# Activation and product of the experts with over 64 tokens, taken before the transpose

## The chip, the cores and the metric

One core of one Trainium2 chip runs the whole program. The metric is the device time of one execution in microseconds (us). The kernel before takes 1499.08 us, the median of three runs (1498.29 to 1501.63). PE is TensorE, ACT is ScalarE, DVE is VectorE, POOL is GpSimd and SP is SyncE.

## What is computed

The reference is a decoder trunk of two layers on 256 tokens of width 1024. Each layer has a mixer (gated linear attention beside a state-space part) and a feed-forward part: dense in layer 0, and in layer 1 eight experts of which every token uses two. The change touches the experts alone:

```python
def swiglu(t, w_gate, w_up, w_down):
    return (jax.nn.silu(t @ w_gate) * (t @ w_up)) @ w_down

def moe_swiglu(h, router_w, w_gate, w_up, w_down):
    ...
    for e in range(N_EXPERTS):
        out = out + gates[:, e:e + 1] * swiglu(t, w_gate[e], w_up[e], w_down[e])
```

`w_gate` and `w_up` of an expert are 1024 x 3584, `w_down` is 3584 x 1024, all float32.

## The kernel before

Products run in float32 accuracy out of split operands: a value is held as a high part and a low part, and PE multiplies high by high, low by high and high by low. So each weight that a DMA brings has to be split: ACT copies the high part (line 182) and DVE subtracts it for the low part (line 183), on tiles of 128 x 2048 elements, one megabyte. One such tile is an *item* here.

An expert's hidden width of 3584 is worked through in seven chunks of 512 columns. A chunk takes six items: two of the gate (G), two of the up projection (U), and two of the down projection (D), which belong to the chunk before, for its hidden values are ready only then. `moe_order` gives this order, G G U U D D. For each item `whole` takes the split weights, `mm_slots` issues the matmuls, `done` gives the buffers back, and `fill` inside it records the splits of a later item on ACT and DVE. Ten buffers of the split weights hold five items, so ACT and DVE work up to five items ahead of PE. Unsplit weights have seven buffers of their own by then, which SP's DMA queue refills when DVE has finished with one (line 154 issues the loads).

Every engine runs its own queue in the order in which the program was written. An engine waits at an instruction, and all that stands behind it waits too.

The tokens of an expert stand in slots, up to 128 of them. Which tokens go where is known only at run time, and so is their count. With at most 64 tokens (*narrow*) the slots hold high and low parts side by side and two matmuls do for three; with more (*wide*) three are issued. `modal` (lines 1192 to 1200) writes both versions into the program as the bodies of `tc.If` and its Else, and a register of PE, ACT and DVE chooses between them. The registers are loaded for PE, ACT and DVE in `is_narrow`.

G and U accumulate in PSUM with slots as rows and hidden columns as columns; D needs them the other way round. So after the second item of G or U, four things follow for each chunk, put by `put` behind certain items:

- `copy` (behind the last G and the last U item): ACT copies the accumulator to a tile `gs` or `us` in SBUF (line 1249).
- `gate` (behind the last U item): PE turns `gs` in four 128 x 128 pieces into `pt`, in a wide expert by transposes (line 1259), in a narrow one by a product with `fold`, which also adds the high and low rows (line 1257). ACT writes silu of it to `fsg` (line 1277).
- `hidden` (two items later): PE turns `us` likewise into `mm`; DVE multiplies it into `fsg` (line 1287).
- `parted` (one item later): ACT copies the high part of `fsg` into `fth` (line 1297), and DVE subtracts for the low part (line 1298).

`at` puts other work between the items: the gathering of the next expert's tokens, the combination of the last expert's output.

Of the kernel before, what the change touches and what calls it, by code (L numbers as in the profile page):

```python
# [8 lines left out]
F = mybir.dt.float32  # L9
# [4 lines left out]
AF = mybir.ActivationFunctionType  # L14
OP = mybir.AluOpType
AX = mybir.AxisListType

P = 128
# [4 lines left out]
FC = 512  # L23
# [8 lines left out]
HALF = P // 2  # L32
# [18 lines left out]
def trunk(ctx: ExitStack, tc: tile.TileContext, a: dict, out: bass.AP):  # L51
    nc = tc.nc
    pe, dve, act, pool, sp = nc.tensor, nc.vector, nc.scalar, nc.gpsimd, nc.sync

    const = ctx.enter_context(tc.tile_pool(name="const", bufs=1))
# [7 lines left out]
    def nm(s):  # L63
        uid[0] += 1
        return f"{s}_{uid[0]}"

    def ps_mm():
        return psum.tile([P, 512], F, name=nm("mm"), tag="mm", bufs=3)

    def ps_t():  # L70
        return psum.tile([P, 512], F, name=nm("pt"), tag="t", bufs=1)
# [6 lines left out]
    def ps_pair():  # L78
        turn[0] ^= 1
        return [ps_y(turn[0]), ps_y(turn[0])]  # L80
# [252 lines left out]
    pe.transpose(pt[:, :DK], c_rows, ident[:DK, :DK])  # L333
    act.activation(s_col, pt[:, :DK], AF.Silu)

    tri = const.tile([P, P], F, name="tri")
    dve.tensor_scalar(tri, jp, 0.0, None, op0=OP.is_ge)
    btri = const.tile([P, P], F, name="btri")
    dve.tensor_scalar(btri, jp, 0.0, 1.0 / 16.0, op0=OP.is_ge, op1=OP.mult)
    dve.memset(btri[0:64, 64:128], 0.0)  # L340
    bmask = btri.bitcast(I32)
# [850 lines left out]
    def modal(narrow, body):  # L1192

        if narrow is None:
            body(False)
        else:
            with tc.If(narrow == 1) as cmp:
                body(True)
            with cmp.Else():
                body(False)  # L1200
# [38 lines left out]

    def run_experts(mo, experts, operand, fold, at):  # L1240

        gs, us, sil, th, ys, ops = {}, {}, {}, {}, {}, {}
        due, ps = {}, {}
        order = list(moe_order(experts))
        where = {t: n for n, t in enumerate(order)}

        def copied(tag, p):
            out = mo.tile([P, FC], F, name=nm(tag), tag=tag)
            act.activation(out, p, AF.Copy)  # L1249
            return out  # L1250

        def folded(src, nar, p):

            for k in range(4):
                ks = slice(k * P, (k + 1) * P)
                if nar:
                    pe.matmul(p[:, ks], src[:, ks], fold, start=True, stop=True)
                else:
                    pe.transpose(p[:, ks], src[:, ks], ident)
            return p  # L1260

        def blocks(t, nar):
            return t.rearrange("p (k t) -> p k t", k=4)[:, :, :HALF if nar else P]

        def put(n, f, *args):
            due.setdefault(n, []).append((f, args))

        def copy(kind, key):
            (gs if kind == "G" else us)[key] = copied("gs" if kind == "G" else "us", ps.pop((kind,) + key))

        def gate(key):
            src, p = gs.pop(key), ps_t()
            s = sil[key] = mo.tile([P, FC], F, name=nm("fsg"), tag="fsg")

            def body(nar):
                folded(src, nar, p)
                act.activation(blocks(s, nar), blocks(p, nar), AF.Silu)

            modal(ops[key[0]][2], body)

        def hidden(key):
            src, p, s = us.pop(key), ps_mm(), sil[key]

            def body(nar):
                folded(src, nar, p)
                sv = blocks(s, nar)
                dve.tensor_tensor(sv, blocks(p, nar), sv, op=OP.mult)

            modal(ops[key[0]][2], body)

        def parted(key):
            t = th[key] = mo.tile([P, 4, P, 2], R, name=nm("fth"), tag="fth", bufs=2)
            s = sil.pop(key)

            def body(nar):
                sv, tv = blocks(s, nar), t[:, :, :HALF if nar else P]
                act.activation(tv[:, :, :, 0], sv, AF.Copy)
                dve.tensor_tensor(tv[:, :, :, 1], sv, tv[:, :, :, 0].bitcast(F), op=OP.subtract)

            modal(ops[key[0]][2], body)  # L1300

        for n, (kind, e, c, i) in enumerate(order):
            key = (e, c)
# [22 lines left out]
            modal(narrow, lambda nar: mm_slots(dsts, nar))  # L1326
            done()
            if kind in "GU" and i:
                put(n, copy, kind, key)
            if (kind, i) == ("U", 1):  # L1330
                lag = 1 if key == (experts[-1], NFC - 1) else 2
                put(n, gate, key)
# [54 lines left out]
    def moe(mo, ys, row, mT):  # L1387
# [8 lines left out]
        pr = mo.tile([P, 2, 2], F, name="pr")  # L1396
# [11 lines left out]
        pool.memset(onesb, 1.0)  # L1408
        iota_s = mo.tile([P, P], F, name="iota_s")
        pool.iota(iota_s, pattern=[[1, P]], base=0, channel_multiplier=0, allow_small_or_imprecise_dtypes=True)  # L1410
        iota_h = mo.tile([P, P], F, name="iota_h")
        pool.iota(iota_h, pattern=[[1, HALF], [0, 2]], base=0, channel_multiplier=0, allow_small_or_imprecise_dtypes=True)
        fold = mo.tile([P, P], F, name="fold")
        pool.iota(fold, pattern=[[-2, P]], base=0, channel_multiplier=1, allow_small_or_imprecise_dtypes=True)
        pm2 = mo.tile([P, 2, P], F, name="pm2")
        dve.tensor_scalar(pm2[:, 0], fold, 0.0, None, op0=OP.is_ge)
# [5 lines left out]
        key = mo.tile([P, NE], F, name="key")  # L1422
# [318 lines left out]

        acc = fnw = None
        y = run_experts(mo, list(range(NE)), lambda e: (xg[e % 2],) + narrow[e], fold, at)
        extra.remove("xm")
        sq, write = finisher(fnw)
# [109 lines left out]
    with tc.tile_pool(name="ffn", bufs=1) as fp:  # L1855
# [4 lines left out]
        ys = [ps_pair(), ps_pair()]  # L1860
# [14 lines left out]
    with tc.tile_pool(name="moe", bufs=1) as mo:  # L1875
        moe(mo, py, g1, mT)
# [23 lines left out]
```

## Time and profile before

| | |
|---|---|
| runs | 1499.08 us median, 1498.29 to 1501.63 |
| the profiled execution | 1499.08 us, of which the span is 1497.3 us |
| mean granted clock of PE | 0.984 |
| busy share of the span | PE 93%, DVE 86%, ACT 70%, POOL 3% |
| read from HBM | 480.12 MB, 321 GB/s over the span |

The span is the time from the first to the last recorded instruction of the profiled execution, so 1.8 us of its time lie outside it. Busy times of different instructions of one engine overlap at their ends, and ends of matmuls are modelled, so a share of 93% or 100% does not say that the engine could do no more. The experts' stage begins near 570 us and ends at the end. In the trace each expert can be told by its lines: 1257 is run in narrow experts only, 1259 in wide ones only.

### The profile page before, as it was taken

The numbers are of one execution on the slowest core, as the hardware profiler recorded it, in microseconds if no ns is written. First come the engines' busy times: TensorE is split into PE (matmuls) and PEld (weight loads), VectorE is DVE, ScalarE is ACT, GpSimd is POOL, SyncE is SP. The second block draws the span as 40 slices with busy tenths as digits, with TensorE's granted clock in tenths as the row PEclk, the third lists the DMA queues.
The fourth block names the chain that finished last, engine by engine and source line by source line (L and its number), as shares of the span: only waits on it lengthen the run. The fifth ranks groups of instructions, "written<-read, shape, count | busy, mean of one in ns | idle before, by whom it ended". The sixth has DMA issues, their size and how long they took to land.

```text
span 1497.3 us, 22117 instructions
## 1 busy us (share of the span) xinstructions
PE 1399.2 (93%) x7578; PEld 1197.3 (80%) x7578; DVE 1289.2 (86%) x1186; ACT 1051.8 (70%) x1255; POOL 46.0 (3%) x72
## 2 busy tenths in 40 slices
PE   4998899999999997999999999999999999998986
PEld 3876699999879776878888778888787888877765
DVE  7898877777766659999889999888999988999996
ACT  3474644544557557898778888778898778888875
POOL 2011000000010011000000000000000000000001
PEclk9999999999999999999999999999999999999998
DMA  9974778888854456999999999999999999999993
GB/s 335 302 259 142 260 268 310 320 314 316 297 176 141 146 175 221 344 395 392 394 340 371 392 392 395 393 348 366 391 393 392 394 371 361 387 393 395 392 393 143
DMA packets 204618, 483.29 MB, mean 323 GB/s; under 512 B 13119, under 2 KB 15405, under 8 KB 204462
## 3 DMA queue, kind: packets, MB, share of 16 engines
q1 hardware_dynamic: 203890, 480.05, 87.3%
q8 instruction: 99, 1.62, 0.4%
q10 hardware_dynamic: 428, 0.63, 0.1%
q0 software_dynamic: 144, 0.52, 0.1%
q14 instruction: 57, 0.47, 0.1%
HBM read 480.12 MB, written 1.05 MB: 321 GB/s over the span
## 4 chain that ended last, share of the span: by engine, by line
PE 70%; DVE 11%; DMA 7%; issue 6%; ACT 5%; POOL 1%; DVEq 0%; ACTq 0%; POOLq 0%
PE mm L1213 10%; PE y L1213 6%; PE mm L1209 5%; PE mm L1210 5%; PE mm L1207 5%; PE mm L429 4%; PE mm L430 4%; PE mm L428 4%; PE y L428 3%; PE y L430 3%; PE y L429 3%; PE y L1207 3%; PE y L1209 3%; DVE ws L183 3%; PE y L1210 3%
## 5 line engine op out<-in xcount | busy, mean ns | idle before, releaser
L174 ACT ACTIVATE ws<-raw 128x1024 fp32r<-128x1024 f32 x136 | 143.8, 1061 | 135.4 <-PE mm L430 62.5
L183 DVE TENSOR_TENSOR ws<-raw,ws 128x2048 fp32r<-128x2048 f32 x97 | 221.4, 2284 | 16.5 <-ACT ws L182 16.3
L175 DVE TENSOR_TENSOR ws<-raw,ws 128x1024 fp32r<-128x1024 f32 x136 | 164.3, 1221 | 55.9 <-ACT ws L174 55.5
L182 ACT ACTIVATE ws<-raw 128x2048 fp32r<-128x2048 f32 x97 | 185.7, 1915 | 25.6 <-PE mm L1210 12.4
L1209 PE MATMUL mm<-ws,hTl 128*128 128x512 f32 x336 | 134.9, 402 | 0.0
L1210 PE MATMUL mm<-ws,hTl 128*128 128x512 f32 x336 | 132.5, 394 | 0.0
L1207 PE MATMUL mm<-ws,hTh 128*128 128x512 f32 x448 | 124.2, 399 | 4.9 <-ACT gs L1249 2.7
L1213 PE MATMUL y<-ws,fth 128*128 128x512 f32 x448 | 126.4, 405 | 0.0
L1213 PE MATMUL mm<-ws,hTl 128*128 128x512 f32 x448 | 122.1, 394 | 0.0
L1213 PE MATMUL mm<-ws,hTh 128*128 128x512 f32 x448 | 121.2, 392 | 0.0
L367 DVE SCALAR_TENSOR_TENSOR ada<-raw,s_col,ada 128x1024 f32<-128x1024 f32 (+1 forms) x98 | 114.4, 1167 | 2.1
L183 DVE TENSOR_TENSOR ws<-xm,ws 128x2048 fp32r<-128x2048 f32 x46 | 105.1, 2285 | 11.5 <-ACT ws L182 11.3
L183 DVE TENSOR_TENSOR ws<-xx,ws 128x2048 fp32r<-128x2048 f32 x47 | 107.3, 2284 | 8.8 <-ACT ws L182 8.7
L183 DVE TENSOR_TENSOR ws<-ada,ws 128x2048 fp32r<-128x2048 f32 x47 | 107.4, 2285 | 7.5 <-ACT ws L182 6.9
L183 DVE TENSOR_TENSOR ws<-xce,ws 128x2048 fp32r<-128x2048 f32 x47 | 107.3, 2284 | 6.6 <-ACT ws L182 6.5
L183 DVE TENSOR_TENSOR ws<-q,ws 128x2048 fp32r<-128x2048 f32 x47 | 107.3, 2283 | 4.4 <-ACT ws L182 3.9
L428 PE MATMUL mm<-hTh,ws 128*128 128x256 f32 x384 | 108.1, 281 | 0.0
L429 PE MATMUL mm<-hTh,ws 128*128 128x256 f32 x384 | 106.9, 278 | 0.0
L430 PE MATMUL mm<-hTl,ws 128*128 128x256 f32 x384 | 106.9, 278 | 0.0
L1213 PEld LDWEIGHTS y<-ws,fth 128*128 128x128 f32 x448 | 88.9, 198 | 19.7
L182 ACT ACTIVATE ws<-q 128x2048 fp32r<-128x2048 f32 x47 | 90.1, 1917 | 16.0 <-PE mm L1210 7.1
L182 ACT ACTIVATE ws<-xx 128x2048 fp32r<-128x2048 f32 x47 | 90.1, 1917 | 16.0 <-PE mm L1210 4.9
(391 smaller groups left out, 3272.5 us busy)
## 6 DMA issues: line engine op xcount, KB each, us to landing
raw<-in_ada_w SPq DMA_DIRECT2D x48, 1024.0 KB, 5.7
raw<-in_moe_w_up SPq DMA_DIRECT2D x33, 1024.0 KB, 6.9
raw<-in_moe_w_gate SPq DMA_DIRECT2D x32, 1024.0 KB, 9.6
raw<-in_moe_w_down SPq DMA_DIRECT2D x32, 1024.0 KB, 12.3
raw<-in_w_in SPq DMA_DIRECT2D x21, 1024.0 KB, 5.3
ada<-in_moe_w_down SPq DMA_DIRECT2D x17, 1024.0 KB, 9.4
xx<-in_moe_w_gate SPq DMA_DIRECT2D x16, 1024.0 KB, 8.1
q<-in_moe_w_gate SPq DMA_DIRECT2D x16, 1024.0 KB, 12.9
```

What stands on the lines that cost most here:

```text
L174: act.activation(h, src, AF.Copy)
L175: dve.tensor_tensor(lo, src, h.bitcast(F), op=OP.subtract)
L182: act.activation(h, r, AF.Copy)
L183: low = lambda: dve.tensor_tensor(lo, r, h.bitcast(F), op=OP.subtract)
L367: dve.scalar_tensor_tensor(acc, w, s_col[:, k:k + 1], acc, op0=OP.mult, op1=OP.add)
L428: pe.matmul(ps, xh, wh, start=start, stop=False)
L429: pe.matmul(ps, xl, wh, start=False, stop=False)
L430: pe.matmul(ps, xh, wl, start=False, stop=stop)
L1207: pe.matmul(ps, xs[:, 0:HALF].rearrange("p s two -> p (s two)"), wh, start=start, stop=False)
L1209: pe.matmul(ps, xs[:, :, 0], wh, start=start, stop=False)
L1210: pe.matmul(ps, xs[:, :, 1], wh, start=False, stop=False)
L1213: pe.matmul(ps, both if nar else xs[:, :, 0], wl, start=False, stop=stop)
```

## The change

In a wide expert silu is taken and the product is formed with slots as rows, straight out of the accumulators, and one tile is transposed where two were. `gate_rows` and `up_rows` take the place of `copy`: behind the last G item ACT writes silu of the accumulator to `gs`, and behind the last U item DVE multiplies the accumulator of U by `gs` into a new tile `prod`. `gate` does nothing in a wide expert. `hidden` transposes `prod`, and `parted` splits it out of PSUM, which `hid` holds until then. In a narrow expert the same instructions run as before, but each step now stands in a `modal`, so that there are two more of these in each chunk. Two constant tiles, `iota_h` and `fold`, take the place of `tri` and `btri`, which are no longer needed by then, for room.

```diff
@@ -333,9 +333,9 @@
     pe.transpose(pt[:, :DK], c_rows, ident[:DK, :DK])
     act.activation(s_col, pt[:, :DK], AF.Silu)
 
-    tri = const.tile([P, P], F, name="tri")
+    tri = const.tile([P, P], F, name="tri", tag="tri")
     dve.tensor_scalar(tri, jp, 0.0, None, op0=OP.is_ge)
-    btri = const.tile([P, P], F, name="btri")
+    btri = const.tile([P, P], F, name="btri", tag="btri")
     dve.tensor_scalar(btri, jp, 0.0, 1.0 / 16.0, op0=OP.is_ge, op1=OP.mult)
     dve.memset(btri[0:64, 64:128], 0.0)
     bmask = btri.bitcast(I32)
@@ -1239,15 +1239,10 @@
 
     def run_experts(mo, experts, operand, fold, at):
 
-        gs, us, sil, th, ys, ops = {}, {}, {}, {}, {}, {}
+        gs, us, sil, hid, prod, th, ys, ops = {}, {}, {}, {}, {}, {}, {}, {}
         due, ps = {}, {}
         order = list(moe_order(experts))
         where = {t: n for n, t in enumerate(order)}
-
-        def copied(tag, p):
-            out = mo.tile([P, FC], F, name=nm(tag), tag=tag)
-            act.activation(out, p, AF.Copy)
-            return out
 
         def folded(src, nar, p):
 
@@ -1265,35 +1260,54 @@
         def put(n, f, *args):
             due.setdefault(n, []).append((f, args))
 
-        def copy(kind, key):
-            (gs if kind == "G" else us)[key] = copied("gs" if kind == "G" else "us", ps.pop((kind,) + key))
+        def gate_rows(key):
+
+            p = ps.pop(("G",) + key)
+            t = gs[key] = mo.tile([P, FC], F, name=nm("gs"), tag="gs")
+            modal(ops[key[0]][2], lambda nar: act.activation(t, p, AF.Copy if nar else AF.Silu))
+
+        def up_rows(key):
+
+            p, g = ps.pop(("U",) + key), gs[key]
+            t = us[key] = mo.tile([P, FC], F, name=nm("us"), tag="us")
+            w = prod[key] = mo.tile([P, FC], F, name=nm("pr"), tag="prod")
+
+            def body(nar):
+                if nar:
+                    act.activation(t, p, AF.Copy)
+                else:
+                    dve.tensor_tensor(w, p, g, op=OP.mult)
+
+            modal(ops[key[0]][2], body)
 
         def gate(key):
             src, p = gs.pop(key), ps_t()
-            s = sil[key] = mo.tile([P, FC], F, name=nm("fsg"), tag="fsg")
+            s = sil[key] = mo.tile([P, 4, HALF], F, name=nm("fsg"), tag="fsg")
 
             def body(nar):
-                folded(src, nar, p)
-                act.activation(blocks(s, nar), blocks(p, nar), AF.Silu)
+                if nar:
+                    folded(src, nar, p)
+                    act.activation(s, blocks(p, nar), AF.Silu)
 
             modal(ops[key[0]][2], body)
 
         def hidden(key):
-            src, p, s = us.pop(key), ps_mm(), sil[key]
+            src, w, s = us.pop(key), prod.pop(key), sil[key]
+            p = hid[key] = ps_mm()
 
             def body(nar):
-                folded(src, nar, p)
-                sv = blocks(s, nar)
-                dve.tensor_tensor(sv, blocks(p, nar), sv, op=OP.mult)
+                folded(src if nar else w, nar, p)
+                if nar:
+                    dve.tensor_tensor(s, blocks(p, nar), s, op=OP.mult)
 
             modal(ops[key[0]][2], body)
 
         def parted(key):
             t = th[key] = mo.tile([P, 4, P, 2], R, name=nm("fth"), tag="fth", bufs=2)
-            s = sil.pop(key)
+            s, p = sil.pop(key), hid.pop(key)
 
             def body(nar):
-                sv, tv = blocks(s, nar), t[:, :, :HALF if nar else P]
+                sv, tv = s if nar else blocks(p, nar), t[:, :, :HALF if nar else P]
                 act.activation(tv[:, :, :, 0], sv, AF.Copy)
                 dve.tensor_tensor(tv[:, :, :, 1], sv, tv[:, :, :, 0].bitcast(F), op=OP.subtract)
 
@@ -1326,7 +1340,7 @@
             modal(narrow, lambda nar: mm_slots(dsts, nar))
             done()
             if kind in "GU" and i:
-                put(n, copy, kind, key)
+                put(n, gate_rows if kind == "G" else up_rows, key)
             if (kind, i) == ("U", 1):
                 lag = 1 if key == (experts[-1], NFC - 1) else 2
                 put(n, gate, key)
@@ -1408,9 +1422,9 @@
         pool.memset(onesb, 1.0)
         iota_s = mo.tile([P, P], F, name="iota_s")
         pool.iota(iota_s, pattern=[[1, P]], base=0, channel_multiplier=0, allow_small_or_imprecise_dtypes=True)
-        iota_h = mo.tile([P, P], F, name="iota_h")
+        iota_h = const.tile([P, P], F, name="iota_h", tag="btri")
         pool.iota(iota_h, pattern=[[1, HALF], [0, 2]], base=0, channel_multiplier=0, allow_small_or_imprecise_dtypes=True)
-        fold = mo.tile([P, P], F, name="fold")
+        fold = const.tile([P, P], F, name="fold", tag="tri")
         pool.iota(fold, pattern=[[-2, P]], base=0, channel_multiplier=1, allow_small_or_imprecise_dtypes=True)
         pm2 = mo.tile([P, 2, P], F, name="pm2")
         dve.tensor_scalar(pm2[:, 0], fold, 0.0, None, op0=OP.is_ge)
```

Where one body of a `modal` gives an engine something to do and the other does not, the built program sets an event semaphore in the empty body: it waits until all that this engine has issued so far is finished, and then counts the engine's semaphore up by what the other body would have added. The listings below show that wait at the branch behind it, as `[waits DVE_49]` or `[waits PE_49]`. A row of the bodies stands for the narrow case first, then for the wide one. `L1197` is the branch of `modal`.

DVE behind the last U item of a chunk, before: a split, the branch of `gate` in which DVE has nothing to do, two more splits, and the bodies of `hidden` (`ws` are split weights, `raw`, `ada` unsplit ones).

```order
L183 TENSOR_TENSOR ws_5961<-raw_731_5674,ws_5960 128x2048 [waits DMAHW4_49,PE_49,Activation_49]
L1197 COMPARE_AND_BRANCH
L1197 UNCONDITIONAL_BRANCH x4
L183 TENSOR_TENSOR ws_6003<-ada_5706,ws_6002 128x2048 [waits DMAHW5_49,PE_49,Activation_49]
L183 TENSOR_TENSOR ws_6030<-raw_739_5733,ws_6029 128x2048 [waits DVE_49,DMAHW6_49,PE_49,Activation_49]
L1197 COMPARE_AND_BRANCH
L1287 TENSOR_TENSOR fsg_5969<-mm_6035,fsg_5969 128x4x64 [waits DVE_49,PE_49]
L1197 UNCONDITIONAL_BRANCH
L1287 TENSOR_TENSOR fsg_5969<-mm_6035,fsg_5969 128x512 [waits DVE_49,PE_49]
L1197 UNCONDITIONAL_BRANCH x2
```

And now: `up_rows` stands between (the row of line 1279 is the wide body, the branch with the wait above it the narrow one).

```order
L183 TENSOR_TENSOR ws_5960<-raw_733_5672,ws_5959 128x2048 [waits DVE_49,DMAHW4_49,PE_49,Activation_49]
L1197 COMPARE_AND_BRANCH
L1197 UNCONDITIONAL_BRANCH [waits DVE_49]
L1279 TENSOR_TENSOR pr_5966<-mm_5910,gs_5881 128x512
L1197 UNCONDITIONAL_BRANCH
L1197 COMPARE_AND_BRANCH
L1197 UNCONDITIONAL_BRANCH x4
L183 TENSOR_TENSOR ws_6000<-ada_5706,ws_5999 128x2048 [waits DVE_49,DMAHW5_49,PE_49,Activation_49]
L183 TENSOR_TENSOR ws_6027<-raw_741_5733,ws_6026 128x2048 [waits DMAHW6_49,PE_49,Activation_49]
L1197 COMPARE_AND_BRANCH
L1301 TENSOR_TENSOR fsg_5971<-mm_6032,fsg_5971 128x256 [waits DVE_49,PE_49]
L1197 UNCONDITIONAL_BRANCH
L1197 UNCONDITIONAL_BRANCH [waits DVE_49]
```

The multiplication moved up from behind the second D item, two splits earlier, and is in the wide body alone; at its new place the narrow body holds the wait for DVE's own work, and at its old place, line 1301, the wide body holds one.

PE behind the last U item of a chunk of expert 1, before: the last matmuls of U, the bodies of `gate`, and the branch to the first D item.

```order
L1213 MATMUL mm_6761<-ws_6654,hTl_6110 128x512 [waits DVE_49]
L1213 MATMUL mm_6761<-ws_6654,hTl_6110 128x512 x3
L1197 UNCONDITIONAL_BRANCH
L1197 COMPARE_AND_BRANCH
L1257 MATMUL pt_6818<-fold,gs_6759 128x128 [waits PE_49,Activation_49]
L1257 MATMUL pt_6818<-fold,gs_6759 128x128 x3
L1197 UNCONDITIONAL_BRANCH
L1259 MATMUL pt_6818<-ident,gs_6759 128x128 [waits PE_49,Activation_49]
L1259 MATMUL pt_6818<-ident,gs_6759 128x128 x3
L1197 UNCONDITIONAL_BRANCH
L1197 COMPARE_AND_BRANCH
```

And now.

```order
L1213 MATMUL mm_6756<-ws_6648,hTl_6108 128x512 [waits DVE_49]
L1213 MATMUL mm_6756<-ws_6648,hTl_6108 128x512 x3
L1197 UNCONDITIONAL_BRANCH
L1197 COMPARE_AND_BRANCH
L1197 UNCONDITIONAL_BRANCH x2
L1197 COMPARE_AND_BRANCH
L1252 MATMUL pt_6816<-fold,gs_6752 128x128 [waits PE_49,Activation_49]
L1252 MATMUL pt_6816<-fold,gs_6752 128x128 x3
L1197 UNCONDITIONAL_BRANCH
L1197 UNCONDITIONAL_BRANCH [waits PE_49]
L1197 COMPARE_AND_BRANCH
```

The four transposes of the wide body are gone, and the wait of PE for its own matmuls stands in their place, right ahead of the branch to the first D item.

## Rows read from the trace of the kernel before

**Rows 1.** Busy time by stretch: us, busy of each engine (instructions), clock, DMA share, GB/s.

```profile
700.00:800.00 100.00, 100.00 (x473) 84.63 (x472) 85.22 (x56) 75.30 (x63) 0.00 (x0) 1.00 1.00 368
806.00:906.00 100.00, 95.58 (x478) 79.32 (x477) 99.69 (x69) 87.99 (x78) 0.00 (x0) 0.98 1.04 392
1271.00:1371.00 100.00, 97.23 (x485) 81.22 (x484) 97.41 (x68) 85.37 (x76) 0.74 (x1) 0.98 1.04 391
1371.00:1471.00 100.00, 87.98 (x401) 69.95 (x399) 96.73 (x65) 82.00 (x65) 0.00 (x0) 0.95 1.03 390
```

**Rows 2.** Tile gs: instructions that read it, count, duration in ns, first and last start.

```profile
L1257 PE MATMUL pt<-fold,gs x280: 270/275/422, 577.9 to 1474.0; 128*128 128x128 f32 x140
L1259 PE MATMUL pt<-ident,gs x84: 270/272/273, 684.3 to 1256.6; 128*128 128x128 f32 x84
```

**Rows 3.** Waits in 806 to 906 us: us in total, times, longest.

```profile
ACT fth L1297 <- DVE fsg L1287: 10.7, 5, 2.8
PEld pt L1257 <- ACT gs L1249: 6.0, 5, 2.5
DVE ws L183 <- ACT ws L182: 0.2, 1, 0.2
```

**Rows 4.** Timeline of DVE, expert 2: start, us, idle before it in brackets.

```profile
859.79 2.28 DVE L183 TENSOR_TENSOR ws<-xce,ws 128x2048 fp32r<-128x2048 f32 x1
861.99 2.27 DVE L183 TENSOR_TENSOR ws<-raw,ws 128x2048 fp32r<-128x2048 f32 x1
864.19 0.41 DVE L1287 TENSOR_TENSOR fsg<-mm,fsg 128x256 f32<-128x256 f32 x1
```

**Rows 5.** Timeline of PE, expert 1, last U item to first D item.

```profile
699.10 1.09 PE L1213 MATMUL mm<-ws,hTl 128*128 128x512 f32 x4
700.04 0.60 PE L1259 MATMUL pt<-ident,gs 128*128 128x128 f32 x4
700.39 0.49 PE L1209 MATMUL y<-ws,fth 128*128 128x512 f32 x1
700.72 0.40 PE L1210 MATMUL y<-ws,fth 128*128 128x512 f32 x1
```

**Rows 6.** Timeline of DVE at the end, and line 1647: its event semaphores (DVEq is DVE's queue).

```profile
1487.44 0.14 DVE L1646 TENSOR_SCALAR fr<-fss 128x1 f32<-128x1 f32 x1
1487.69 0.31 DVE L1647 SCALAR_TENSOR_TENSOR fr<-fss,fr 128x1 f32<-128x1 f32 x1
...
L1647 DVEq EVENT_SEMAPHORE  x2: 21/21/21, 1487.6 to 1488.7; - x2
```

**Rows 7.** Line 1197 in DVE's queue: whole span, 856.0 to 856.5 us; line 183, 856.4.

```profile
L1197 DVEq COMPARE_BRANCH  x295: 43/47/63, 581.5 to 1479.2; - x148
...
L1197 DVEq COMPARE_BRANCH  x2: 43/45/47, 856.1 to 856.2; - x2
...
L183 DVEq EVENT_SEMAPHORE  x1: 50/50/50, 856.4 to 856.4; - x1
```

**Rows 8.** PE at 609 us: timeline of its weight loads, and line 1197 in its queue.

```profile
609.54 0.40 PEld L1599 LDWEIGHTS y<-ident,pm 128*128 128x128 f32 x2 [0.67 <-DVE pm L1577]
610.14 0.76 PEld L1207 LDWEIGHTS y<-ws,fth 128*128 128x128 f32 x4 [0.20 <-issue]
...
L1197 PEldq COMPARE_BRANCH  x2: 63/118/174, 609.8 to 610.0; - x2
```

**Rows 9.** PE's queue in expert 1: line 1197, and line 1259 behind it.

```profile
L1197 PEldq COMPARE_BRANCH  x1: 207/207/207, 702.8 to 702.8; - x1
...
L1259 PEldq EVENT_SEMAPHORE  x1: 51/51/51, 703.1 to 703.1; - x1
```

**Rows 10.** Timeline around 850 us: a product on DVE, and ACT, which waits for it.

```profile
849.28 0.42 DVE L1287 TENSOR_TENSOR fsg<-mm,fsg 128x256 f32<-128x256 f32 x1
...
849.79 0.44 ACT L1297 ACTIVATE fth<-fsg 128x256 fp32r<-128x256 f32 x1 [2.72 <-DVE fsg L1287]
850.12 1.89 ACT L182 ACTIVATE ws<-xm 128x2048 fp32r<-128x2048 f32 x1
```

## The prediction

> **What bounds the kernel now.** I read the busy time by stretch first, then the waits of one stretch, then the timelines of DVE and PE there. The reader is to see two kinds of stretch in the experts' stage. In wide experts PE is busy 100 of 100 us and DVE 85 [rows 1]; matmuls follow each other every 0.23 us with no gap between items [rows 5]. PE sets the time there. In narrow experts it is DVE: it is busy 99.7 of 100 us [rows 1], waited for ACT once, for 0.2 us [rows 3], and its splits follow each other every 2.20 us, though one takes 2.28 [rows 4]. The others wait behind it: ACT 10.7 us for DVE's product, and PE, through ACT's copy of gs, 6.0 us [rows 3]. The DMA engines look full in both kinds of stretch (share 1.00 to 1.04), but no wait of [rows 3], in the narrow one, is for a DMA, so that a later DVE there makes a later end. There are 84 / 4 = 21 wide chunks, three experts, and 280 / 8 = 35 narrow ones, five experts [rows 2]. The wide ones are experts 1, 3 and 5; 6 and 7 are both narrow and come last.
>
> **What the change removes.** In each wide chunk four transposes. The U item's last four matmuls begin at 699.10, the transposes 0.94 us later, the D item's first matmul 0.35 us after these, and its second one 0.33 us after the first where the last four of U stand 0.94 / 4 = 0.235 us apart [rows 5]. So four transposes cost 0.35 + 0.10 = 0.45 us of PE, and 21 x 0.45 = 9.45 us if nothing comes in their place. ACT loses a copy and a silu in each wide chunk, and DVE's product moves two items ahead, behind a split that is late anyway; in wide experts both engines have 15 us and more of room in 100 [rows 1], and the transposes of the product come two items later, so I cost this at nothing. What hides it is PE's bound; should DVE be late by more than the two items, PE would wait for the product. The narrow product, copies and folds stay as they are. DMA issues keep their order on SP and POOL.
>
> **What it adds: a wait of DVE for itself.** In a narrow chunk DVE now waits, behind the last U item, until its split has ended, and only then does its queue go on to the jump over the wide body, to the branch of gate with its own jump, and to the waits of the next split. Today the queue does such things while a split of 2.28 us runs, and nobody sees them: a compare or jump takes 43 to 63 ns [rows 7]. Behind a wait they are seen. Four prices, each from a row:
> - Lost overlap of two splits: 2.28 - 2.20 = 0.08 us [rows 4].
> - From the end of an instruction over an event semaphore that waits for it to the next start: 1487.58 to 1487.69, 0.11 us [rows 6].
> - A compare, a jump and the next entry of the queue: 856.1, 856.2 and 856.4, so 0.1 us for a compare that falls through and 0.2 for a jump that is taken [rows 7]. In the queue stand a jump, a compare and a jump: 0.5 us.
> - One more event semaphore ahead of the split, some 0.1 us by the same rows (an estimate from 0.11).
>
> Together 0.08 + 0.11 + 0.5 + 0.1 = 0.79, say 0.8 us. The lower bound is the wait alone, 0.19. For the upper one I take each entry at half as much again, 1.1. ACT's queue passes the branch behind its product and starts the next split 0.33 us behind the product's start [rows 10], which speaks for a smaller price, but that queue works beside an instruction of 0.44 us; I stay with DVE's own rows.
>
> All of DVE's time counts in experts 0, 2 and 4: 3 x 7 x 0.8 = 16.8 us. In experts 6 and 7, DVE has 2.6 and 3.3 us idle in 200 us [rows 1], a part of it waiting for weights; the delay uses this up first: 14 x 0.8 - 5.9 = 5.3 us.
>
> [...]
>
> **And a wait of PE for itself.** In a wide chunk the transposes' place is taken by a wait of PE for its own last matmul, with the branch to the D item behind it. The last of the four matmuls ends at 699.10 + 1.09 = 700.19 [rows 5]. From there: an instruction that waited for another engine starts some 0.09 us behind the end of what it waited for (ACT at 849.79, behind a product that ends at 849.28 + 0.42 = 849.70), the event semaphore takes 0.05 and its handing on some 0.02 [rows 9, 10], and a compare that jumps to the wide body has the next entry behind it after 0.3 us, nearer 0.27 by its length of 0.207 [rows 9]. That is 0.43, and the D item's first matmul begins at about 700.64, where it begins at 700.39 now: 0.25 us later, without the transposes. So what was removed is more than paid back. A second row bears this out: where PE's two small transposes at 609 us came late, the second weight load started at 609.80 and the D item's at 610.14, with a jump and a compare between, and 0.20 us of the time is put down to issue [rows 8]. Bounds: if only the 0.09 is seen, 0.11 us are won per chunk; with the branch at twice its price 0.5 us are lost. 21 x 0.25 = 5.2 us.
>
> **The sum.** 16.8 + 5.3 + 5.2 = +27.3 us. The profiled execution took 1499.08 us, 1497.3 of it the span; it is the median run itself, so the sum stands against either: 1526 us. With all prices at their lower bounds it is 21 x 0.19 - 21 x 0.11 = +1.7 us, with all at their upper ones 21 x 1.1 + (14 x 1.1 - 5.9) + 21 x 0.5 = +43 us.
>
> **Rivals.**
> - *Faster: waits of an engine for itself cost nothing.* Then the four transposes are won whole: 1499.1 - 9.45 = 1489.6 us. The point from which it decides is on PE: it wins only by as much as the next matmul starts sooner than 0.20 us behind the end of the last (700.39 - 700.19). For it: an engine runs its instructions in order anyway, and DVE's end-to-start is only 0.11 us [rows 6]. Against it: 0.08 us of overlap go in any case, and the entries behind the wait are in the rows. [...] 0.06.
> - *No change: only the waits are seen, the branches run ahead.* 0.19 on DVE and -0.11 on PE: +1.7 us, 1500.8. 0.08.
> - *Narrow experts are paced by the DMA engines, not DVE.* Their share is 1.04 there [rows 1]. Then DVE's delay is free in all of them, and PE's is left: +5.2 us, 1504.3. Against it: ACT, which reads the weights first, waits for DVE in [rows 3], and no wait there is for a DMA. 0.08.
> - *The entries of the queues cost half.* DVE's 0.6 us of them become 0.3, its delay 0.49; PE's branch costs 0.14 less, its delay 0.11: 21 x 0.49 + (14 x 0.49 - 5.9) + 21 x 0.11 = +13.6 us, 1512.7. For it speaks ACT's row [rows 10]. 0.18.
>
> That the change doesn't do what it says is no rival: the listing shows the transposes gone and both waits in place.
>
> **How the numbers follow.** The forecast has 0.60, the rivals 0.06, 0.08, 0.08 and 0.18. The range takes in the forecast but for its uppermost bounds, and the last two rivals, and leaves out the first two: 1504 to 1537 us, about 0.8. A measurement of this kernel can tell 0.2%, 3.0 us, from no change: faster 0.06, same 0.08, slower 0.86.
>
> **What the profile after would show.** If right: in wide chunks a gap of PE ahead of the first D matmul, which stands 700.39 - 699.10 = 1.29 us behind the first of the last four U matmuls now and would stand 1.54 behind it; in narrow chunks a gap of some 0.7 us on DVE behind the split that follows the last U item, put down to issue or to nothing; the time from product to product of expert 2, 864.19 - 849.28 = 14.91 us [rows 4, 10], 0.8 us longer; DMA share below 1.04 there. The prediction is wrong if DVE's narrow stretches show no such gap, if the gap is there and the experts are no longer for it, or if the D item's first matmul stands 1.29 us or less behind the U item's.

## The result and the profile after

The changed kernel takes 1525.79 us, the median of four runs, against 1499.93 us for the kernel before in as many: a ratio of 1.0178 (95% interval 1.0165 to 1.0190). It is slower by 25.9 us; 27 had been forecast. The profiled execution took 1528.11 us, with a span of 1526.3. Two executions, 2803 us of the kernel before and 2783 us of a later one (e9_fold), lie far outside all others and are in no ratio below.

Busy time by stretch, after, columns as in [rows 1]:

```profile
540.00:580.00 40.00, 37.20 (x198) 33.05 (x197) 27.02 (x50) 23.77 (x31) 1.12 (x2) 0.83 0.37 131
700.00:800.00 100.00, 97.78 (x444) 80.94 (x443) 85.25 (x58) 69.45 (x52) 0.00 (x0) 1.00 0.97 351
806.00:906.00 100.00, 95.55 (x471) 79.27 (x471) 94.17 (x64) 83.28 (x74) 0.00 (x0) 0.98 1.03 382
1371.00:1471.00 100.00, 90.93 (x411) 73.52 (x409) 95.50 (x67) 78.39 (x64) 0.74 (x1) 0.93 1.04 393
```

In the wide stretch PE falls from 100 to 97.8, in the narrow one DVE from 99.7 to 94.2: where each engine was the bound, it now has holes, and the clock in these two stretches is what it was (1.00 and 0.98). The holes stand where the listing had put the waits. The timeline of DVE in expert 2, and ACT beside it:

```profile
862.86 0.42 DVE L1301 TENSOR_TENSOR fsg<-mm,fsg 128x256 f32<-128x256 f32 x1
...
871.15 2.30 DVE L183 TENSOR_TENSOR ws<-q,ws 128x2048 fp32r<-128x2048 f32 x1
874.21 2.29 DVE L183 TENSOR_TENSOR ws<-xce,ws 128x2048 fp32r<-128x2048 f32 x1 [0.76 <-ACT ws L182]
876.42 2.29 DVE L183 TENSOR_TENSOR ws<-raw,ws 128x2048 fp32r<-128x2048 f32 x1
878.62 0.42 DVE L1301 TENSOR_TENSOR fsg<-mm,fsg 128x256 f32<-128x256 f32 x1
...
870.32 1.92 ACT L182 ACTIVATE ws<-xce 128x2048 fp32r<-128x2048 f32 x1
```

The brackets name ACT, but ACT's split of that tile ended at 870.32 + 1.92 = 872.24, two microseconds before DVE starts. What DVE did in the gap is in its queue, line 1197 (the branch and the wait in the empty body) and line 183 (the waits of the split itself):

```profile
L1197 DVEq COMPARE_BRANCH  x3: 43/47/47, 873.6 to 873.8; - x3
L1197 DVEq EVENT_SEMAPHORE  x1: 21/21/21, 873.5 to 873.5; - x1
...
L183 DVEq EVENT_SEMAPHORE  x2: 21/36/50, 874.0 to 874.1; - x2
```

The split ends at 873.45. The wait passes at 873.5, three branches follow from 873.6 to 873.8, two event semaphores at 874.0 and 874.1, and the next split starts at 874.21. PE in expert 1, with its queue:

```profile
708.57 1.09 PE L1213 MATMUL mm<-ws,hTl 128*128 128x512 f32 x4
710.12 0.51 PE L1209 MATMUL y<-ws,fth 128*128 128x512 f32 x1 [0.46 <-PEq L1197]
710.47 0.39 PE L1210 MATMUL y<-ws,fth 128*128 128x512 f32 x1
...
L1197 PEldq COMPARE_BRANCH  x2: 210/210/210, 709.9 to 710.2; - x2
L1197 PEldq EVENT_SEMAPHORE  x1: 51/51/51, 709.7 to 709.7; - x1
```

The four transposes of [rows 5] are gone, and the first D matmul stands 710.12 - 708.57 = 1.55 us behind the first of the last four U matmuls, where it stood at 1.29.

How much each expert lost is read from ACT, whose first write of `gs` in each marks its begin. For expert 1 and the one behind it, before and then after:

```profile
680.78 0.58 ACT L1249 ACTIVATE gs<-mm 128x512 f32<-128x512 f32 x1
806.44 0.58 ACT L1249 ACTIVATE gs<-mm 128x512 f32<-128x512 f32 x1
```

```profile
689.50 0.58 ACT L1267 ACTIVATE gs<-mm 128x512 f32<-128x512 f32 x1
817.08 0.58 ACT L1267 ACTIVATE gs<-mm 128x512 f32<-128x512 f32 x1
```

So 125.66 us before and 127.58 after. Worked out in the same way for all, from one profiled execution of each kernel (the last part reaches to the end of the span; the names are those of the experiments below):

| us | narrow 0, 2, 4 | wide 1, 3, 5 | 6, 7 to the end | sum |
|---|---|---|---|---|
| before | 313.8 | 377.9 | 228.4 | 920.0 |
| after | 330.7 | 383.4 | 231.5 | 945.6 |
| e6_idle | 329.5 | 375.3 | 233.6 | 938.4 |
| e1_tiny | 315.1 | 383.1 | 228.3 | 926.4 |
| e5_one | 325.6 | 382.0 | 228.3 | 935.9 |
| e3_gate | 330.0 | 368.5 | 228.8 | 927.2 |
| e8_before_gate | 319.3 | 375.1 | 227.7 | 922.1 |
| e2_splits | 315.3 | 383.2 | 228.5 | 927.0 |
| e4_both | 319.7 | 369.0 | 228.5 | 917.2 |
| e7_tiny_gate | 318.9 | 368.9 | 228.9 | 916.8 |
| e9_fold | 315.7 | 369.1 | 228.7 | 913.5 |
| e10_copy | 316.6 | 370.2 | 229.0 | 915.9 |
| e11_no_wait_dve | 315.2 | 370.7 | 229.5 | 915.4 |
| e12_no_wait | 314.7 | 368.8 | 228.1 | 911.6 |

The span grew by 29.0 us (1526.3 - 1497.3), the sum of this table by 25.5. The other 3.4 were lost ahead of the experts, in code whose work the change leaves alone. The mean clock differs there: 0.83 was granted from 540 to 580 us in the first row above, and 0.96 in the kernel before:

```profile
540.00:580.00 40.00, 35.02 (x207) 30.71 (x207) 28.82 (x49) 26.04 (x33) 1.12 (x2) 0.96 0.40 140
```

The experts began between 576.9 and 582.1 us in the fourteen traces, the kernel before at 577.3. The median run after is 2.3 us shorter than the profiled one. So the table is the closer measure of what an edit of the experts does, and medians are held against it. It is one execution of each kernel, though: the first D matmul of a wide chunk stands 1.29 us behind the first of the last four U matmuls in the kernel before, in e6_idle and in e8_before_gate alike, and their wide experts take 377.9, 375.3 and 375.1 us. Differences of 2 to 3 us in one column tell nothing by themselves.

### The profile page after: what moved, and what is told of

It reads as the page before. It is cut to its first block, busy times and chain, and to the rows that moved or that the text cites. A ratio compares the mean times of both kernels' runs of the same rounds, so it can differ in the third digit from the quotient of the medians.

```text
span 1526.3 us, 22692 instructions
## 1 busy us (share of the span) xinstructions
PE 1412.8 (93%) x7494; PEld 1200.8 (79%) x7494; DVE 1292.9 (85%) x1186; ACT 1029.5 (67%) x1213; POOL 44.4 (3%) x72
## 5 line engine op out<-in xcount | busy, mean ns | idle before, releaser
L1207 PE MATMUL mm<-ws,hTh 128*128 128x512 f32 x448 | 125.9, 403 | 2.2 <-ACT hTh L508 2.2
L1213 PE MATMUL mm<-ws,hTh 128*128 128x512 f32 x448 | 122.6, 396 | 0.0
```

Source lines behind the costliest of these rows:

```text
L1207: pe.matmul(ps, xs[:, 0:HALF].rearrange("p s two -> p (s two)"), wh, start=start, stop=False)
L1213: pe.matmul(ps, both if nar else xs[:, :, 0], wl, start=False, stop=stop)
```

## The experiments

Each ratio is that of the kernel's runs to those of the kernel before on the same chip, with its 95% interval.

### DVE's wait alone, in the kernel before

```diff
+        def idle_body(key):
+            w = mo.tile([P, 1], F, name=nm("one"), tag="one")
+            def body(nar):
+                if not nar:
+                    dve.memset(w, 0.0)
+            modal(ops[key[0]][2], body)
...
             if (kind, i) == ("U", 1):
...
+                put(n, idle_body, key)
                 put(n, gate, key)
```

> The kernel before, with one more modal behind the last U item: nothing in the narrow body, a memset of a 128x1 column on DVE in the wide one. So DVE waits for itself in narrow chunks as in the changed kernel, and nothing else is changed. Theory: the same gap of some 0.76 us in narrow chunks, 21 x 0.85 = 17.9 us in experts 0, 2 and 4, some 3 us in 6 and 7, nothing in wide ones: 1500 + 20 = 1520 us. Rival A (DMA engines pace the narrow experts): 1500 us. Rival B (only the wait is seen, 0.19 us): 1504 us.

Measured (e6_idle): 1518.96 us, ratio 1.0140 (1.0120 to 1.0160). Timeline of DVE in expert 2:

```profile
865.38 2.28 DVE L183 TENSOR_TENSOR ws<-q,ws 128x2048 fp32r<-128x2048 f32 x1
868.36 2.29 DVE L183 TENSOR_TENSOR ws<-xce,ws 128x2048 fp32r<-128x2048 f32 x1 [0.69 <-ACT ws L182]
```

The narrow experts 0, 2 and 4 take 15.8 us more, of 17.9 expected, 6 and 7 5.2 us, of 3 expected, and the wide ones lose nothing (375.3 against 377.9). No value is computed differently in this kernel, so the wait, with the branches behind it, alone makes most of the loss of the change. With the DMA engines as the bound of the narrow experts it would have been free; that rival falls.

### DVE's wait taken away

```diff
                 if nar:
                     act.activation(t, p, AF.Copy)
+                    dve.memset(w[:, 0:1], 0.0)
                 else:
                     dve.tensor_tensor(w, p, g, op=OP.mult)
```

> The narrow body of up_rows also gets one DVE instruction, a memset of a 128x1 column of the product's tile, so that DVE has work in both bodies and needs not wait for itself there. Theory (the wait of DVE for itself in narrow chunks costs 0.85 us a chunk, as the gap in the trace after): the gap of 0.76 us behind the split goes, about 0.1 to 0.15 us for the memset comes (an estimate from the 0.14 us of a 128x1 instruction), so about 20 us are given back but for 2 to 5: 1506 to 1511 us. Rival A (the time goes to the added branches, which stay, on three engines): no change, 1525 us. Rival B (DMA engines pace the narrow experts): no change either, though the gap on DVE goes.

Measured (e1_tiny): 1506.06 us, ratio 1.0044 (1.0029 to 1.0060). The branches are still there, and the narrow experts are back at 315.1 us (313.8 before); the wide ones keep their 383.1. The memset added nothing:

```profile
861.04 2.28 DVE L183 TENSOR_TENSOR ws<-xx,ws 128x2048 fp32r<-128x2048 f32 x1
...
865.45 2.28 DVE L183 TENSOR_TENSOR ws<-xce,ws 128x2048 fp32r<-128x2048 f32 x1
865.47 0.06 DVE L1278 MEMSET pr<- 128x1 f32 x1
867.66 2.28 DVE L183 TENSOR_TENSOR ws<-raw,ws 128x2048 fp32r<-128x2048 f32 x1
...
L1197 DVEq COMPARE_BRANCH  x4: 43/45/47, 861.8 to 862.2; - x4
```

The next split follows the last by 2.21 us, against 2.20 in the kernel before, so the branches of the two modals, four entries of the queue, cost nothing where no wait precedes them: the queue takes them from 861.8 to 862.2, while an earlier split runs.

The same without an added instruction: the split that DVE makes there anyway (`split_whole` defers it) is written into both bodies.

```diff
+            state["apart"] = last_u
             done()
+            state["apart"] = False
...
+                up_rows(key, held[0::2])
...
             def body(nar):
+                for low in splits:
+                    low()
```

> The split that DVE makes behind the last U item is put into both bodies of up_rows (ahead of the product in the wide one), so that DVE has work in both and no instruction is added to narrow chunks. Theory: as the memset of one column in the other experiment, the gap on DVE goes; narrow experts 0, 2 and 4 take 105.4 us as in the kernel before, wide ones keep PE's wait and 127 to 128 us: 1506 us. Rival (a split that stands behind a branch starts late, since its queue cannot pass the branch before the last split is under way): 0.2 to 0.5 us a chunk, 1511 to 1518 us.

Measured (e2_splits): 1506.66 us, ratio 1.0051 (1.0034 to 1.0068), and columns in the table within 0.3 us of those with the memset. The rival, a split that is late behind its branch, falls.

### Fewer branches behind the wait

```diff
+        def rows_and_gate(key):
+            first, second = up_rows(key), gate(key)
+            modal(ops[key[0]][2], lambda nar: (first(nar), second(nar)))
...
+                    put(n, rows_and_gate, key)
...
-                put(n, gate, key)
```

> up_rows and gate stand in one modal instead of two; both waits, DVE's in narrow and PE's in wide chunks, stay, but DVE has one jump and one compare fewer behind its wait. Theory (0.5 us of DVE's delay are entries of its queue behind the wait): the gap on DVE falls from 0.76 to about 0.5 us, and a chunk of the narrow experts 0, 2 and 4 takes 0.26 us less: 21 x 0.26 + 2 = 7 us, 1518 to 1519 us. Rival (the wait alone makes the gap, the entries run ahead): gap and time stay, 1525 us.

Measured (e5_one): 1518.58 us, ratio 1.0121 (1.0104 to 1.0138). DVE in expert 2, timeline and queue:

```profile
873.69 2.29 DVE L183 TENSOR_TENSOR ws<-xce,ws 128x2048 fp32r<-128x2048 f32 x1 [0.50 <-PE mm L1213]
...
L1197 DVEq EVENT_SEMAPHORE  x1: 21/21/21, 873.2 to 873.2; - x1
L1197 DVEq COMPARE_BRANCH  x1: 47/47/47, 873.3 to 873.3; - x1
```

One branch is left of three, the gap falls from 0.76 to 0.50 us, and experts 0, 2 and 4 take 5.1 us less, of 5.5 expected. So the two entries that went, a jump and a compare that falls through, cost 0.26 us together. They do not cost the same: in the trace after, the entries behind the wait begin at 873.59 (jump), 873.77 (compare), 873.85 (jump) and 874.05 (event semaphore), so that a jump takes 0.18 to 0.20 us until the next entry and the compare 0.07.

### PE's wait taken away

```diff
-            modal(ops[key[0]][2], body)
+            return body
...
-            modal(narrow, lambda nar: mm_slots(dsts, nar))
+            if (kind, i) == ("U", 1):
+                turn_gate = gate(key)
+                modal(ops[e][2], lambda nar: (mm_slots(dsts, nar), turn_gate(nar)))
+            else:
+                modal(narrow, lambda nar: mm_slots(dsts, nar))
...
-                put(n, gate, key)
```

> The body of gate is put at the end of the bodies of the last U item, so that PE has matmuls in both bodies and needs not wait for itself in wide chunks; narrow chunks keep DVE's wait. Theory (PE's wait with the branch behind it costs 0.26 us a chunk over what the four transposes cost, that is 0.26 + 0.45 = 0.71 us in all): the first D matmul stands 0.85 to 0.95 us behind the first of the last four U matmuls in wide chunks, where it stands 1.55 behind in the trace after, and 21 x 0.7 = 15 us are given back: 1511 us. Rival A (wide experts are longer because the product comes earlier or its accumulator is held longer, not for PE's wait): the matmuls move up, but the wide experts stay as long, 1525 us. Rival B (DVE or ACT, with waits of their own in wide chunks, become the bound there): a part of it, about 1518 us.

Measured (e3_gate): 1506.15 us, ratio 1.0036 (1.0021 to 1.0052). PE in expert 1:

```profile
708.33 1.09 PE L1213 MATMUL mm<-ws,hTl 128*128 128x512 f32 x4
709.26 0.39 PE L1209 MATMUL y<-ws,fth 128*128 128x512 f32 x1
```

The D item follows 0.93 us behind the first of the last four U matmuls, and the wide experts take 383.4 - 368.5 = 14.9 us less, just as expected. The time is 5 us below the expectation. The edit also saves a modal, which I had not counted: DVE has two branches fewer behind its wait, and its gap is 0.50 us in this trace too. But in the table that gives back only 0.7 us in experts 0, 2 and 4, not the 5.1 of the last experiment, and 2.7 in 6 and 7; expert 0 even takes 2.1 us more. The edit moves something else as well, which the next run shows.

The same edit in the kernel before, where PE has no such wait:

> The kernel before, with gate's body at the end of the last U item's bodies, one modal less in each chunk and nothing else changed. Theory (a modal whose bodies leave no engine to wait for itself costs nothing, and the gain of the two cured kernels is the transposes'): 1499 us, within 2 us of the kernel before. Rival (the branches of a modal cost the bound engine time even without a wait): 56 x 0.1 to 0.3 us less, 1483 to 1494 us.

Measured (e8_before_gate): 1505.70 us, ratio 1.0041 (1.0025 to 1.0058): slower, which neither theory had. Of the 6.5 us by which its span is longer, 4.5 lie ahead of the experts, which begin at 581.8 us and not at 577.3; in the experts 2.1 are lost. There the narrow experts 0, 2 and 4 lose 5.5 us, and the wide ones take 2.7 less, as in e6_idle. ACT early in expert 0, and DVE beside it:

```profile
598.87 0.38 ACT L1277 ACTIVATE fsg<-pt 128x256 f32<-128x256 f32 x1 [3.71 <-DVE fth L1298]
599.14 1.90 ACT L182 ACTIVATE ws<-xm 128x2048 fp32r<-128x2048 f32 x1
...
598.33 0.42 DVE L1298 TENSOR_TENSOR fth<-fsg,fth 128x256 fp32r<-128x256 f32 x1
601.08 2.29 DVE L183 TENSOR_TENSOR ws<-xm,ws 128x2048 fp32r<-128x2048 f32 x1 [2.33 <-ACT ws L182]
```

The edit had moved silu (line 1277) ahead of ACT's split of that item. Silu waits for DVE to be done with the last `fsg`, the split now waits behind silu, and DVE waits 2.33 us for the split. In the kernel before the split comes first:

```profile
590.43 1.89 ACT L182 ACTIVATE ws<-xm 128x2048 fp32r<-128x2048 f32 x1
...
594.39 0.38 ACT L1277 ACTIVATE fsg<-pt 128x256 f32<-128x256 f32 x1 [1.60 <-DVE fth L1298]
```

Expert 0 takes 2.4 us more for it.

### Both waits taken away

The split in both bodies and gate moved:

> Both cures: the split in both bodies of up_rows for DVE, and gate at the end of the last U item's bodies for PE. Theory (the two waits are all that the change lost, and four transposes a wide chunk all that it won): narrow experts as before, 105.4 us, wide ones 122.8 us as in the run with gate moved alone, against 125.7 before: 1499.6 - 21 x 0.45 = 1490 us. Rival A (with PE free of the wait, ACT's two waits for itself or DVE's one in wide chunks set their time): wide experts over 124 us, 1494 us or more. Rival B (the gain of the run with gate moved came in part from the modal that it saves): see the kernel before with gate moved alone.

Measured (e4_both): 1500.31 us, ratio 1.0016 (0.9999 to 1.0033). The memset and gate moved:

> As the run with both cures, but DVE's is the memset of one column in the narrow body. Theory: the memset costs nothing beside the split, 1490 us, the same as with the split in both bodies. Rival (the place of the split in the bodies matters): 2 us or more between the two.

Measured (e7_tiny_gate): 1496.22 us, ratio 0.9979 (0.9963 to 0.9994). Wide experts are at 369 us in both, 8.9 us below the kernel before, and narrow ones 5 to 6 us above it; the moved silu is to account for that, which the next kernel tries. By the table the two kernels differ by 0.4 us, by their medians by 4.1, where the rival had asked for 2 or more; what makes that difference stays open.

Then with only the products with `fold` moved, and silu left behind the split, in the narrow body of `up_rows`:

```diff
                     folded(src, nar, p)
-                    act.activation(s, blocks(p, nar), AF.Silu)
...
+            folds.append(lambda: act.activation(s, blocks(p, True), AF.Silu))
+            return body
...
-            modal(narrow, lambda nar: mm_slots(dsts, nar))
+            turn_gate = gate(key) if (kind, i) == ("U", 1) else lambda nar: None
+            modal(narrow, lambda nar: (mm_slots(dsts, nar), turn_gate(nar)))
...
+            silu = folds.pop()
...
                 if nar:
                     act.activation(t, p, AF.Copy)
+                    silu()
+                    dve.memset(w[:, 0:1], 0.0)
```

> Both cures, with ACT's order as in the kernel before: only gate's products with fold stand at the end of the last U item's bodies, and silu stands behind the copy in the narrow body of up_rows, behind the split of that item; DVE has the memset of one column there. Theory (the runs with gate's whole body moved lost some 3 us in expert 0 and more in the chunks at the ends of experts because silu stood ahead of ACT's split and held it up): expert 0 takes 103.5 us again, wide ones 122.5 to 123.2, and the time is 1499.3 - 9.45 = 1490 us, or up to 1494 where wide experts that end earlier leave the narrow ones behind them waiting for their weights. Rival (the loss is the DMA engines': the stage reads its weights no faster whatever PE saves): 1495 to 1500 us, with ACT's waits for DMAs grown by as much as the wide experts got shorter.

Measured (e9_fold): 1496.04 us, ratio 0.9972 (0.9959 to 0.9985). The table has narrow experts at 315.7 and the sum at 913.5, 6.5 us below before; the median is 4.2 below. Expert 0 takes 104.0 us, 2.7 less than in e7_tiny_gate, and experts 0, 2 and 4 together 3.2 less. So the silu's place is confirmed as the larger part; 1.9 us above the kernel before remain. The time misses 1490 and lies in the range of the rival, the DMA engines. But ACT's waits for DMAs in the experts add up to 18.8 us, against 16.4 in the kernel before, where the rival wanted them grown by the 8.8 us that the wide experts got shorter; so it can explain a part at most. Some of the rest stands in the first chunk of expert 2: 15.15 us, against 14.37 before. In the memset's place a copy of one column:

> The same, with a copy of one column (128x1, gs to the product's tile) in place of the memset. Theory (the memset reads nothing, so it ran beside the split, where its record begins 0.02 us behind the split's start; an instruction that reads takes its turn): 0.06 to 0.14 us a narrow chunk, 2 to 5 us more than with the memset. Rival (any short instruction without a wait hides): within 1 us of it.

Measured (e10_copy): 1494.60 us, ratio 0.9959 (0.9943 to 0.9974).

```profile
857.68 0.14 DVE L1281 COPY pr<-gs 128x1 f32<-128x1 f32 x1
857.74 2.27 DVE L183 TENSOR_TENSOR ws<-xce,ws 128x2048 fp32r<-128x2048 f32 x1
```

It takes 0.06 us until the next start, at the lower end of what was expected; over a program that is 2 us, and the two medians, 1.4 us apart the other way, cannot tell it.

In these kernels DVE still waits for itself in wide chunks, at its old place in `hidden`. In the one with only the products moved, DVE on the border from expert 1 to 2:

```profile
805.29 2.29 DVE L183 TENSOR_TENSOR ws<-q,ws 128x2048 fp32r<-128x2048 f32 x1 [0.61 <-DVEq L1197]
```

A memset in that body too (first piece), and then also a copy of one column for ACT in the wide body of `up_rows` (second piece):

```diff
                 if nar:
                     dve.tensor_tensor(s, blocks(p, nar), s, op=OP.mult)
+                else:
+                    dve.memset(s[:, 0, 0:1], 0.0)
...
                 else:
+                    act.activation(t[:, 0:1], g[:, 0:1], AF.Copy)
                     dve.tensor_tensor(w, p, g, op=OP.mult)
```

> The kernel with both cures and ACT's order kept, and now also a memset of one column on DVE in the wide body of hidden, so that DVE never waits for itself. Theory (DVE's wait in wide chunks is free but in the last ones ahead of a narrow expert, where DVE already splits for that expert: 0.61 us of it stand in the trace at 805 us, three times in the program): the first chunk of expert 2 takes 14.4 to 14.6 us in place of 15.15, and the time is some 2 us less, 1494 us. Rival A (the narrow experts give back time because their weights come late): no change, 1496 us. Rival B (DVE's waits in wide chunks cost in all of them): wide experts shorter than 122.5 us.

> The same, and ACT copies one column in the wide body of up_rows, so that no engine waits for itself in any body of the experts. Theory (ACT's wait in wide chunks delays the split behind it by about 0.5 us, which counts in the chunk ahead of a narrow expert alone): 0 to 1.5 us less than without it, 1492 to 1494 us. Rival (ACT is never late there): within 0.5 us of the run without it.

Measured: 1494.26 us, ratio 0.9952 (0.9935 to 0.9969) (e11_no_wait_dve), and 1493.95 us, ratio 0.9952 (0.9935 to 0.9969) (e12_no_wait). DVE on the border in the first of them:

```profile
799.41 2.29 DVE L183 TENSOR_TENSOR ws<-xx,ws 128x2048 fp32r<-128x2048 f32 x1 [0.42 <-ACT ws L182]
801.65 0.06 DVE L1307 MEMSET fsg<- 128x1 f32 x1
801.71 2.29 DVE L183 TENSOR_TENSOR ws<-q,ws 128x2048 fp32r<-128x2048 f32 x1
```

The gap is gone, though the memset takes its turn here: the splits stand 2.30 us apart, not 2.20. The first chunk of expert 2 takes 14.93 us (14.4 to 14.6 expected), and the sums of the table, 915.4 and 911.6 around the 913.5 of the kernel without the edits, vary by more than the edits were to give. What waits of the engines off the bound cost is therefore not settled; by the ratios, 0.9972 without these edits and 0.9952 with them, it could be 3 us, which their intervals do not tell from nothing. The last kernel, in which no engine waits for itself, is faster than the kernel before by 6.5 us by the medians and 8.4 us in the table, of the 9.45 that the four transposes were worth.

## Why the prediction was right

- **The bounds.** DVE's wait, put into the kernel before, costs narrow experts alone (15.8 us in 0, 2 and 4 and 5.2 in 6 and 7, with the wide ones at 375.3 against 377.9); PE's, taken out of the changed one, gives back 14.9 us in the wide experts, which DVE's cure alone leaves at 383.1. Both steps hold.
- **DVE's price, 0.8 us.** Measured 0.85: a gap of 0.76, and the overlap of 0.08 lost. Product to product it is 878.62 - 862.86 = 15.76 us against 14.91. The terms, by the times of the queue: from the split's end to the first branch 0.14 us, where 0.11 stood for the wait; the three branches 0.46, put at 0.5; the event semaphores ahead of the split 0.16, put at 0.1. Small errors nearly cancel. Experts 0, 2 and 4 lost 17.0 us, where 16.8 stood in the sum, and that close a fit is in part luck: the wait gives back 15.6 us of it when it is taken away and costs 15.8 when it is put into the kernel before. Some 1.3 us (315.1 against 313.8) stay without it, and no run shows what they are.
- **The branches behind the wait.** Behind DVE's wait a jump takes 0.18 to 0.20 us until the next entry, where [rows 7] had given 0.2, and a compare that falls through 0.07, where they had given 0.1; the entries of PE's compare that jumps are 0.21 us long in the trace after. With the event semaphores that follow, DVE's entries make 0.46 + 0.16 = 0.62 us of its gap of 0.76, so the rival by which they cost half, 0.3, falls.
- **The wait itself.** The row of the queue has it pass 0.05 us behind the split's end (873.5 against 873.45); most of the loss is the overlap of 0.08 us and what stands behind the wait.
- **PE's price, 0.25 us.** Measured 0.26 (1.55 against 1.29), and 5.5 us in the three wide experts against 5.2. The working has a slip that does not matter: 0.43 us behind 700.19 is 700.62, not 700.64, so 0.23 and 4.8 us. Without the wait the D item stands at 0.93, so the transposes' 0.36 + 0.10 us were rightly counted: with the wait gone the wide experts take 9.4 us less than before, 0.45 a chunk. PE's wait costs 0.62 us to D's first matmul and 0.71 a chunk by the table.
- **Experts 6 and 7: the mis-sized term.** 5.3 us stood in the sum, 3.1 were lost, all of it in 6; expert 7 to the end took 0.6 us less than before. The 5.9 us of idle time were read from windows that end at 1471 us. Added up to the end of the span, the gaps ahead of DVE's instructions are 2.6 us in expert 6 and 8.7 in expert 7 before, 5.6 and 9.2 after: in 7 seven waits were added and the gaps grew by 0.5 us, so nearly all of the delay fell into time that DVE waited anyway. But in e6_idle, with the same waits, the two experts lost 5.2 us; why the rest of the change gives some 2 us back there is not shown.
- **The rest at nothing.** ACT's and DVE's moved work in wide chunks costs nothing that shows: with both waits gone the wide experts come out 8.9 us shorter, of 9.45.

The sum was 27.3; the table gives 17.0 + 5.5 + 3.1 = 25.5 with rounding, the medians 25.9.

## What to carry to other kernels

Before a step goes into one side of a run-time branch, look at what each engine does on the other side: in these programs a side on which an engine has nothing makes it wait for all its own work, and then the branches that the queue takes during a split in e1_tiny (861.8 to 862.2) are paid in full, 0.46 us of DVE's gap of 0.76. The loss stood on the engine that is the bound: 15.6 us for DVE's wait in experts 0, 2 and 4, 14.9 for PE's in 1, 3 and 5, while the waits of DVE and ACT in wide chunks, where PE is the bound, made no difference that the table can tell (915.4 and 911.6 us without them, 913.5 with them). A one-column memset or a piece of that engine's own next work in the empty side removed DVE's (experts 0, 2 and 4 at 315.1 and 315.3 us, from 330.7). When a body is moved to cure one engine's wait, see what it moves on the other engines' queues: silu ahead of a split cost 3.2 us by the kernel that puts it back, 5.5 by the one in which gate alone moves, of some 9 that the four transposes had brought.

## What the runs showed of the hardware

A memset of 128x1 in front of a split of 2.28 us has a record that begins 0.02 us behind the start of that split, though it stands ahead of it in the program, and adds nothing in e1_tiny (2.21 us from split to split); in e11_no_wait_dve, where the memset itself has a semaphore to wait for, it takes its turn and adds 0.1 us (2.30). A copy of the same size takes its turn and adds 0.06 us (e10_copy). That the memset hides because it reads nothing was my estimate and is not shown: the one that takes its turn reads nothing either. Behind a wait of DVE for itself a jump takes 0.18 to 0.20 us until the queue's next entry, a compare that falls through 0.07 (trace after, 873.59 to 874.05). The gap behind a wait of DVE for itself is put down in the trace to ACT, to PE or to the queue (0.76, 0.50 and 0.61 us above), whichever semaphore the next split also waits for; only the queue's own rows tell what it was. And the code ahead of the experts ran at a mean granted clock of 0.83 in one execution and 0.96 in another between 540 and 580 us: 13.6 and 3.4 of the 40 us were at a granted clock of 0.50. The experts began 3.4 us later in the first (580.7 against 577.3). How much of this the clock made is not shown, for in e12_no_wait they began at 581.1 us with 0.96 there.
